# Feed-forward weights from one list in order of use, token sums in the second product, tables one step per block

## The chip, the cores and the metric

The kernel runs on one core of a Trainium2 chip. The metric is the device time of one execution in microseconds (us). A core has a matrix engine (PE, with its weight loads PEld), a vector engine (DVE), a scalar engine (ACT), a general engine (POOL) and an engine that here only issues transfers (SP); each takes its instructions strictly in order, and they meet at semaphores.

## What is computed

Two hybrid layers (a gated delta rule beside sliding-window attention, then a feed-forward part), followed by a state-space block; 512 tokens, width 1024, all in fp32. The change touches the feed-forward part and the tables of the state-space block. Of the reference this is what matters:

```python
D_MODEL, SEQ, DEPTH, D_FF = 1024, 512, 2, 4 * 1024

def hybrid_layer(x, ...):
    ...
    x = x + rmsnorm(mix, post_mix_g)
    h2 = rmsnorm(x, pre_mlp_g)
    ff = jnp.square(jax.nn.relu(h2 @ w_ff1)) @ w_ff2
    return x + rmsnorm(ff, post_mlp_g)
```

The state-space block later needs tables of powers of a complex number per state (exponentials, sines, rotations) that depend on its parameters alone. They can be made at any time before, and the kernel makes half of them beside each layer's feed-forward part.

## The kernel before

**Precision.** Each fp32 operand is split into a high and a low part (`wh`/`wl` for weights, `xsh`/`xsl` for the normed input, `hh`/`hl` for the hidden layer), and a product is three matrix multiplications, high by high, low by high and high by low (`mm3`, L78). For a weight tile of 512 KB that is one transfer from DRAM into `raw` or `raws`, one cast on ACT (L191 or L252) and one subtraction on DVE (L192 or L253). `wh` and `wl` are rings of three, `raw` and `raws` of two each. Kept weights are called `kw`.

**Stages of a feed-forward part.** The 4096 hidden columns come in four blocks of eight columns of 128 (`gidx`); for each block the first product makes the hidden columns, and the second product adds their share to `acc`. In layer 0 the part runs from about 618 to 1000 us of the trace, in layer 1 from about 1612 to 1995.

- Block 0 begins while the residual of the part before still runs: its first six columns (`NFF`) are made in two token halves (`dense_half`, 24 multiplications of 256 columns each), all six for the first half of the tokens, then all six for the second. The second halves need the normed input `xsh`/`xsl` of the second token half, which comes from the residual: load `xo` (SP), `rt` (DVE, POOL), write `xd_mid` (SP), `xsh` (ACT), `xsl` (DVE). Columns 6 and 7 are made as a fast pair.
- A fast pair (`fast_pair`) makes two columns with seven half products in place of eight. It needs sums of weights, formed in `load_pair` on POOL (L257 to L261), each then cast (L252) and subtracted (L253), and sums of tokens `ta`, `tb` (`token_sums`), formed once per layer beside the six second halves. Its results are added up on DVE (`y`, L280).
- Blocks 1 to 3 make their eight columns in four fast pairs each. Blocks 0 to 2 then run the second product over all 512 tokens (`dense2` for two columns, `dense` for six), block 3 in token halves with the residual that follows; its first five weight columns are kept for the second half.

**Tables.** `ssm_tables` is a generator of 38 steps, advanced twice per pair and once per column of a second product. Its prologue loads `row`, `dt` (two transfers of 2 KB in 4-byte pieces), `lbr`, `lbi`; then come an exponential of `dt` on ACT (L1047, with a load of the activation table before it), small DVE steps, seven steps on POOL (six operations of 128x128 each, L1000 to L1005), transposes, loads of `crow` with transposes on PE (L81), and eight steps on DVE (L1000 to L1005).

**What sets the order.** A scheduler takes the instructions in the order in which the program issues them and the buffers' state, and writes one list per engine. All transfers go through SP's queue, on eight semaphores in turn, so a transfer also waits for the one eight places ahead of it.

Of the kernel before, what the change touches and what calls it, by code (L numbers as in the profile page):

```python
# [19 lines left out]
P = 128  # L20
SEQ = 512
# [5 lines left out]
SKIP, KEPT, LATE, FREE, HPOOL = 2, 5, (5, 6, 7, 0, 1, 2, 3, 4), (3, 0, 0, 0), (((0, 0), (1, 0), (2, 0), (3, 0)), ())  # L27
# [27 lines left out]
def body(  # L55
# [118 lines left out]

    def load_w(src, kn=KD, n=P, pool_h=False, keep=None):
        turn[0] += 1
        if turn[0] % 3 == 2 and turn[1] is not None and turn[0] > turn[2]:
            raw = turn[1].tile([P, kn, n], F32, tag="rawx", name="rawx", bufs=1)
        else:
            raw = raw_tile() if kn == KD and n == P else wp.tile([P, kn, n], F32, tag="raw", name="raw", bufs=2)  # L180
# [30 lines left out]
    def dense2(ws, xs):  # L211
        ps = [ps_mm() for _ in ws]
        kn = len(xs)
        order = (*range(kn - 2), kn - 1, kn - 2)
        for ks in (order[:-2], order[-2:]):
            for p, (h, lo) in zip(ps, ws):
                for k in ks:
                    mm3(p, h[:, k, :], lo[:, k, :], *xs[k], k == order[0], k == order[-1])
        return ps
# [18 lines left out]
    def load_pair(src, c, pool):  # L238


        r0, r1 = raw_tile(), raw_tile()
        for j, r in enumerate((r0, r1)):
            DMA.dma_start(out=r, in_=src[:, (c + j) * P:(c + j + 1) * P].rearrange("(k p) n -> p k n", p=P))
        a1, a2 = slice(0, 4), slice(4, 8)
        s1 = pool.tile([P, 4, P], F32, tag="s1", name="s1", bufs=1)

        def parts(raw):
            if raw is s1:
                h, lo = [pool.tile([P, 4, P], F32R, tag=nm, name=nm, bufs=1) for nm in ("sh", "sl")]
            else:  # L250
                h, lo = [wp.tile([P, KD, P], F32R, tag=nm, name=nm, bufs=3) for nm in ("wh", "wl")]
            S.copy(out=h, in_=raw)  # L252
            V.tensor_tensor(out=lo, in0=raw, in1=f32(h), op=ALU.subtract)  # L253
            return h, lo

        d = parts(r0)
        G.tensor_tensor(out=s1, in0=r1[:, a1], in1=r1[:, a2], op=ALU.add)  # L257
        G.tensor_tensor(out=r1[:, a1], in0=r0[:, a1], in1=r1[:, a1], op=ALU.subtract)
        x = parts(r1)
        G.tensor_tensor(out=r0[:, a1], in0=s1, in1=r0[:, a1], op=ALU.subtract)  # L260
        G.tensor_tensor(out=r0[:, a2], in0=r0[:, a2], in1=r0[:, a1], op=ALU.subtract)  # L261
        return d, x, parts(r0), parts(s1)

# [1443 lines left out]
```

## Time and profile before

| | |
|---|---|
| median of 3 runs | 2347.36 us (2345.46 to 2352.49) |
| the profiled execution | 2347.78 us |
| its span | 2346.1 us |
| PE busy | 2241.6 us (96%) |
| DVE, ACT, POOL busy | 1517.7, 955.5, 629.1 us |
| mean granted clock of PE | 0.983 |

The profiled execution is 0.4 us above the median, and 1.7 us of it lie outside the span. A busy PE is not PE at full rate: where the clock is 0.50 a multiplication takes twice as long, and the engine still counts as busy.

### The profile page before, as it was taken

The numbers are of one execution on the slowest core, as the hardware profiler recorded it, in microseconds if no ns is written. First come the engines' busy times: TensorE is split into PE (matmuls) and PEld (weight loads), VectorE is DVE, ScalarE is ACT, GpSimd is POOL, SyncE is SP. The second block draws the span as 40 slices with busy tenths as digits, with TensorE's granted clock in tenths as the row PEclk, the third lists the DMA queues.
The fourth block names the chain that finished last, engine by engine and source line by source line (L and its number), as shares of the span: only waits on it lengthen the run. The fifth ranks groups of instructions, "written<-read, shape, count | busy, mean of one in ns | idle before, by whom it ended". The sixth has DMA issues, their size and how long they took to land. (4 is left out here: it accounts for less than half of the span.)

```text
span 2346.1 us, 37815 instructions
## 1 busy us (share of the span) xinstructions
PE 2241.6 (96%) x14532; PEld 1953.5 (83%) x14532; DVE 1517.7 (65%) x2976; ACT 955.5 (41%) x1734; POOL 629.1 (27%) x683
## 2 busy tenths in 40 slices
PE   8999999999989999999999999999899999899998
PEld 7877888888978888988778888789788899877788
DVE  5579793446677685665797934467776866544645
ACT  4454333233543353444543333335433434424333
POOL 1644320200417123246443202004271232200001
PEclk9999999999989999999999999999999999999999
DMA  6232424665442433342223345654434324554344
GB/s 178 57 78 83 96 81 128 178 205 168 140 111 84 119 109 94 107 138 59 73 83 93 94 127 181 201 158 140 111 92 120 112 73 140 175 162 121 100 135 144
DMA packets 466432, 284.34 MB, mean 121 GB/s; under 512 B 48502, under 2 KB 440012, under 8 KB 465740
## 3 DMA queue, kind: packets, MB, share of 16 engines
q1 hardware_dynamic: 464848, 281.74, 41.4%
q8 instruction: 114, 1.87, 0.3%
q14 instruction: 66, 0.54, 0.1%
q10 hardware_dynamic: 1404, 0.19, 0.1%
HBM read 235.76 MB, written 46.11 MB: 120 GB/s over the span
## 5 line engine op out<-in xcount | busy, mean ns | idle before, releaser
L78 PE MATMUL psm<-xsh,wh 128*128 128x512 f32 (+1 forms) x1104 | 431.9, 392 | 1.4 <-ACT xsh L307 1.0
L78 PE MATMUL psm<-xsl,wh 128*128 128x512 f32 (+1 forms) x1104 | 418.7, 379 | 4.3 <-DVE xsl L310 3.9
L78 PE MATMUL psm<-xsh,wl 128*128 128x512 f32 (+1 forms) x1104 | 419.0, 380 | 0.0
L192 DVE TENSOR_TENSOR wl<-raw,wh 128x1024 fp32r<-128x1024 f32 (+2 forms) x207 | 252.9, 1222 | 110.3 <-ACT wh L191 81.8
L191 ACT CAST wh<-raw 128x1024 fp32r<-128x1024 f32 (+2 forms) x154 | 152.9, 993 | 316.8 <-PE psm L78 254.9
L78 PEld LDWEIGHTS psm<-xsh,wh 128*128 128x128 f32 x1104 | 210.3, 191 | 44.5 <-issue 7.6
L78 PEld LDWEIGHTS psm<-xsl,wh 128*128 128x128 f32 x1104 | 210.9, 191 | 40.3 <-DVE xsl L310 4.6
L78 PEld LDWEIGHTS psm<-xsh,wl 128*128 128x128 f32 x1104 | 210.1, 190 | 40.0 <-issue 0.3
L341 POOL TENSOR_TENSOR sa<-sa,sq 128x256 f32<-128x256 f32 x54 | 51.8, 960 | 659.4 <-ACT sq L336 375.0
L78 PE MATMUL psm<-hh,wh 128*128 128x512 f32 (+1 forms) x480 | 177.6, 374 | 0.0
L78 PE MATMUL psm<-hl,wh 128*128 128x512 f32 (+1 forms) x480 | 176.6, 369 | 0.0
L78 PE MATMUL psm<-hh,wl 128*128 128x512 f32 (+1 forms) x480 | 175.6, 369 | 0.0
L78 PE MATMUL psa<-tb,wh 128*128 128x256 f32 x416 | 82.2, 295 | 25.0 <-ACT wh L252 20.7
L78 PEld LDWEIGHTS psm<-hh,wh 128*128 128x128 f32 x480 | 90.3, 189 | 15.7 <-ACT wh L191 0.8
L78 PEld LDWEIGHTS psm<-hh,wl 128*128 128x128 f32 x480 | 90.5, 188 | 15.2
L78 PEld LDWEIGHTS psm<-hl,wh 128*128 128x128 f32 x480 | 90.5, 189 | 14.9 <-issue 0.8
L189 POOL TENSOR_SCALAR wh<-raw 128x1024 fp32r<-128x1024 f32 (+1 forms) x53 | 61.5, 1162 | 151.7 <-PE psm L78 120.1
L78 PEld LDWEIGHTS psa<-tb,wh 128*128 128x128 f32 x416 | 68.0, 201 | 26.9 <-ACT wh L252 21.5
L78 PE MATMUL psa<-xsh,wh 128*128 128x256 f32 x312 | 89.1, 286 | 0.0
L78 PE MATMUL psa<-xsl,wh 128*128 128x256 f32 x312 | 88.9, 285 | 0.0
L78 PE MATMUL psa<-xsh,wl 128*128 128x256 f32 x312 | 88.9, 285 | 0.0
L78 PE MATMUL psm<-ah,wh 128*128 128x512 f32 x256 | 80.8, 396 | 5.7 <-ACT ah L307 5.2
(672 smaller groups left out, 5726.0 us busy)
## 6 DMA issues: line engine op xcount, KB each, us to landing
raw<-in_w_in_dram SPq DMA_DIRECT2D x130, 512.0 KB, 3.9
raw<-in_w_ff_dram SPq DMA_DIRECT2D x75, 512.0 KB, 4.3
raws<-in_w_ff_dram SPq DMA_DIRECT2D x49, 512.0 KB, 4.0
gate<-dg SPq DMA_DIRECT2D x48, 256.0 KB, 3.8
rawx<-in_w_in_dram SPq DMA_DIRECT2D x14, 512.0 KB, 4.1
raw<-in_w_up_sw_dram SPq DMA_DIRECT2D x12, 512.0 KB, 5.1
raw<-in_w_up_dn_dram SPq DMA_DIRECT2D x11, 512.0 KB, 6.6
raw<-in_w_o_dram SPq DMA_DIRECT2D x10, 512.0 KB, 5.2
```

Source lines behind the costliest of these rows:

```text
L78: return s.issue(nc.tensor.matmul(*a, **k))
L189: G.tensor_scalar(out=h, in0=raw, scalar1=1.0, scalar2=0.0, op0=ALU.mult, op1=ALU.add)
L191: S.copy(out=h, in_=raw)
L192: V.tensor_tensor(out=lo, in0=raw, in1=f32(h), op=ALU.subtract)
L341: (G if s.n in POOL_ACC else V).tensor_tensor(out=s.acc, in0=s.acc, in1=sq, op=ALU.add)
```

## The change

- A class `Weights` holds one list of the feed-forward weights in order of use. It starts the preparation of the next weight (transfer, sums, cast, subtraction) in the program as soon as a place in its ring is released, after the last product that reads it (`free`), where before `load_w` and `load_pair` stood directly before the use. With the list, transfers run up to one item ahead.
- Columns 6 and 7 of block 0 are plain products over all 512 tokens (48 multiplications of 512 columns) and no longer a fast pair (84 of 256 columns).
- The token sums are issued in the second product of block 0, one step per column; their pool is opened after the six columns are done.
- The tables advance once per pair or column, after it, and no longer twice per pair; `crow` is loaded some steps earlier, in two buffers.
- In block 3 the first three columns' weights come from the list; two columns are kept in place of five, so columns 0, 1 and 2 are loaded and split a second time in the second token half, at its end.

```diff
-SKIP, KEPT, LATE, FREE, HPOOL = 2, 5, (5, 6, 7, 0, 1, 2, 3, 4), (3, 0, 0, 0), (((0, 0), (1, 0), (2, 0), (3, 0)), ())
+SKIP, KEPT, LATE, FREE, HPOOL = 2, 5, (5, 6, 7, 3, 4, 0, 1, 2), (3, 0, 0, 0), (((0, 0), (1, 0), (2, 0), (3, 0)), ())
...
+    class Weights:
+        def __init__(s, items):
+            s.items, s.fetched, s.got = list(items), [], []
+            s.steps = [(i, p) for i, (src, pair) in enumerate(s.items) for p in ("dxes" if pair else "w")]
+            s.room = {"ring": 0, "s": 1}
...
+        def fetch(s, upto):
+            while len(s.fetched) <= min(upto, len(s.items) - 1):
+                src, pair = s.items[len(s.fetched)]
+                raw = []
+                for j in range(1 + pair):
+                    raw.append(raw_tile())
+                    DMA.dma_start(out=raw[j], in_=src[:, j * P:(j + 1) * P].rearrange("(k p) n -> p k n", p=P))
+                s.fetched.append(raw)
...
+        def free(s, what):
+            s.room[what] += 1
+            while s.steps and s.room["s" if s.steps[0][1] == "s" else "ring"]:
+                i, p = s.steps.pop(0)
+                s.room["s" if p == "s" else "ring"] -= 1
+                s.fetch(i)
+                s.got.append(s.part(p, s.fetched[i]))
+                if spare[0] is not None and p in "ws":
+                    s.fetch(i + 1)
...
+        def part(s, p, raw):
...
+            elif p == "x":
+                G.tensor_tensor(out=s.s1, in0=raw[1][:, a1], in1=raw[1][:, a2], op=ALU.add)
+                G.tensor_tensor(out=raw[1][:, a1], in0=raw[0][:, a1], in1=raw[1][:, a1], op=ALU.subtract)
+            elif p == "e":
+                G.tensor_tensor(out=raw[0][:, a1], in0=s.s1, in1=raw[0][:, a1], op=ALU.subtract)
+                G.tensor_tensor(out=raw[0][:, a2], in0=raw[0][:, a2], in1=raw[0][:, a1], op=ALU.subtract)
...
+            S.copy(out=h, in_=t)
+            V.tensor_tensor(out=lo, in0=t, in1=f32(h), op=ALU.subtract)
+            return h, lo
...
-        tR = sp.tile([P, NG, 32], F32, tag="crow", name="tR")
+        tR = sp.tile([P, NG, 32], F32, tag="crow", name="tR", bufs=2)
...
+            items = [up(n) for n in range(NFF, KD)]
+            for g in range(4):
+                if g:
+                    items += [up(g * KD + n, 2) for n in range(0, KD, 2)]
+                items += [down(g, n) for n in range(KD if g < 3 else 3)]
+            w = Weights(items)
...
-                            ts = next(sums, None) or ts
+                        if i and n < 3:
+                            w.free("ring")
...
-                    ys = fast_pair(load_pair(w_ff1[l], gidx * KD + len(hid), spare[0]), mid.xs, ts)
-                    for _ in range(2):
-                        next(tables, None)
...
+                    if gidx:
+                        ys = fast_pair(w, mid.xs, ts)
...
+                    else:
+                        ps = dense(w.take(), mid.xs)
+                        w.free("ring")
+                        hid.append(hidden())
+                        relu2(ps, *hid[-1])
+                    next(tables, None)
...
                         if gidx == 0:
                             V.tensor_copy(out=acc[n], in_=ps)
+                            next(sums, None)
...
-                return kp.tile([P, kn, n], F32R, tag="kw", name="kw", bufs=10)
+                return kp.tile([P, kn, n], F32R, tag="kw", name="kw", bufs=4)
...
+                    if i == 0 and n < 3:
+                        wn = w.take()
+                    elif i and j > 4:
+                        wn = load_w(down(3, n)[0])
```

How the order on the engines moves at three places of layer 0 (layer 1 has the same at its place):

On SP, before, the prologue of the tables (`row`, `dt`, `lbr`, `lbi`) stands behind the last loads of the token sums (`tsa`, `tsb`), after the whole residual:

```order
L290 DMA tsa_6712<-xd_mid0_5569 128x512
L290 DMA tsb_6713<-xd_mid0_5569 128x512
L243 DMA raws_6812<-in_w_ff1_dram 128x8x128
L1030 DMA row_6934<-in_ssm_lam_re_2_dram 8x128
L1038 DMA dt_6946<-in_ssm_log_dt_2_dram 64x8x1 x2
L1043 DMA lbr_6949<-in_ssm_b_re_2_dram 64x8x16 x2
L1043 DMA lbi_6950<-in_ssm_b_im_2_dram 64x8x16 x2
L181 DMA raws_6993<-in_w_ff2_dram 128x8x128
```

On SP, after, the same transfers stand within the residual of the second token half, between its fourth load (`xo_6344`) and its first write (`xd_mid0<-rt_6314`), with weight loads between them:

```order
L430 DMA xo_6344<-xd_in_96 128x256
L1059 DMA row_6798<-in_ssm_lam_re_2_dram 8x128
L1067 DMA dt_6810<-in_ssm_log_dt_2_dram 64x8x1 x2
L1072 DMA lbr_6813<-in_ssm_b_re_2_dram 64x8x16
L231 DMA raw_6230<-in_w_ff1_dram 128x8x128
L1072 DMA lbr_6813<-in_ssm_b_re_2_dram 64x8x16
L1072 DMA lbi_6814<-in_ssm_b_im_2_dram 64x8x16
L189 DMA raw_6562<-in_w_ff1_dram 128x8x128
L1072 DMA lbi_6814<-in_ssm_b_im_2_dram 64x8x16
L401 DMA xd_mid0_5569<-rt_6314 128x256
L430 DMA xo_6355<-xd_in_96 128x256
L189 DMA raw_6599<-in_w_ff1_dram 128x8x128
```

So the last four `xo` loads of the residual, and the load `raw_6599` of column 7's weight, now stand behind the prologue.

On ACT, before, the exponential of `dt` stands behind the last eviction of the six columns and ahead of the casts for the fast pair:

```order
L307 CAST hh_6501<-fq_6788 128x256
L277 COPY y0_6924<-psa_6836 128x256
L1047 ACT_TABLE_LOAD
L1047 ACTIVATE dt_6946<-dt_6946 128x8
L252 CAST sh_6832<-s1_6815 128x512
L252 CAST wh_6822<-raws_6812 128x1024
L252 CAST wh_6828<-raw_6811 128x1024
L191 CAST wh_6995<-raws_6993 128x1024
```

On ACT, after, it stands ahead of the first eviction of the six columns (`ft_6263` from `psm_6238`), and so ahead of every `xsh` of the second token half:

```order
L365 ACTIVATE sq_6190<-mo_5568 128x256
L241 CAST kw_6226<-raw_6224 128x1024
L1076 ACT_TABLE_LOAD
L1076 ACTIVATE dt_6810<-dt_6810 128x8
L1380 ACTIVATE ft_6263<-psm_6238 128x256
L1382 ACTIVATE fq_6265<-ft_6263 128x256
L336 CAST hh_6236<-fq_6265 128x256
L241 CAST kw_6232<-raw_6230 128x1024
L1380 ACTIVATE ft_6303<-psm_6278 128x256
L1382 ACTIVATE fq_6305<-ft_6303 128x256
L336 CAST hh_6276<-fq_6305 128x256
L341 ACTIVATE xsh_5922<-rt_6314,prm_91 128x256
```

The exponential has moved over some 45 instructions of ACT, from behind the second halves to ahead of the first.

Further down on ACT, after, the casts of the weights of columns 6 and 7 (`wh_6564`, `wh_6601`) stand among the evictions of the second halves:

```order
L336 CAST hh_6465<-fq_6494 128x256
L1380 ACTIVATE ft_6525<-psm_6500 128x256
L320 ACTIVATE tsa_6983<-tsa_6983,prm_91 128x512
L320 ACTIVATE tsb_6984<-tsb_6984,prm_91 128x512
L1382 ACTIVATE fq_6527<-ft_6525 128x256
L221 CAST wh_6564<-raw_6562 128x1024
L1380 ACTIVATE ft_6556<-psm_6531 128x256
L336 CAST hh_6498<-fq_6527 128x256
L1382 ACTIVATE fq_6558<-ft_6556 128x256
L336 CAST hh_6236<-fq_6558 128x256
L221 CAST wh_6601<-raw_6599 128x1024
```

There, `psm_6531` is the first of the six second halves, so both casts come some five columns ahead of the products that read them.

## Rows read from the trace of the kernel before

**Rows 1.** PE's waits, layer 0, 640 to 1040 us: total us, times, longest.

```profile
PE psa L78 <- ACT wh L252: 11.8, 2, 9.7
...
PE psa L81 <- DMA crow<-in_ssm_c_im_dram: 2.8, 1, 2.8
...
PE psm L78 <- DVE kw L192: 2.4, 1, 2.4
...
PE psa L78 <- DVE y L280: 1.9, 2, 1.5
```

**Rows 2.** PE's waits, layer 1, 1640 to 2060 us.

```profile
PE psa L78 <- ACT wh L252: 8.9, 2, 6.7
...
PE psa L81 <- DMA crow<-in_ssm_c_im_dram: 2.6, 1, 2.6
PE psm L78 <- DVE kw L192: 2.3, 1, 2.3
```

**Rows 3.** Timeline of PE: start, us, instruction, idle before and its releaser.

```profile
668.62 0.79 PE L78 MATMUL psa<-tb,wh 128*128 128x256 f32 x2 [9.66 <-ACT wh L252]
...
1661.58 0.80 PE L78 MATMUL psa<-tb,wh 128*128 128x256 f32 x2 [6.68 <-ACT wh L252]
```

**Rows 4.** Stretches: us, busy time per engine, PEclk, DMA share, GB/s.

```profile
662.00:664.00 2.00, 0.00 (x0) 0.00 (x0) 1.99 (x3) 0.38 (x1) 1.32 (x1) 0.50 0.14 9
...
674.00:676.00 2.00, 2.00 (x16) 2.00 (x16) 0.16 (x1) 1.05 (x1) 0.00 (x0) 0.78 1.05 309
...
820.00:830.00 10.00, 9.50 (x67) 9.53 (x68) 9.34 (x31) 2.37 (x3) 2.22 (x2) 0.83 0.19 54
...
1950.00:1960.00 10.00, 9.82 (x69) 9.82 (x70) 6.36 (x8) 6.43 (x10) 0.00 (x0) 0.83 0.63 185
```

**Rows 5.** Timeline of ACT at the first stall of layer 0.

```profile
663.62 1.28 ACT L1047 ACT_TABLE_LOAD   x1 [4.08 <-DMA dt<-in_ssm_log_dt_dram]
666.90 0.21 ACT L1047 ACTIVATE dt<-dt 128x8 f32<-128x8 f32 x1 [2.00 <-DMA dt<-in_ssm_log_dt_dram]
```

**Rows 6.** Timeline of SP: the last xo loads, then the tables' prologue.

```profile
632.77 0.94 SPq L401 DMA_DIRECT2D xo<-xd_in  x2
...
654.52 1.37 SPq L1038 DMA_DIRECT2D dt<-in_ssm_log_dt_dram  x2
...
657.29 7.80 SPq L1043 DMA_DIRECT2D lbi<-in_ssm_b_im_dram  x2
```

**Rows 7.** Timeline of ACT and of PE where the residual meets the first halves.

```profile
622.01 0.38 ACT L1347 ACTIVATE ft<-psm 128x256 f32<-128x256 f32 x1
...
640.51 0.49 ACT L312 ACTIVATE xsh<-rt,prm 128x256 fp32r<-128x256 f32 x1
...
618.93 0.28 PE L78 MATMUL psm<-xsh,wh 128*128 128x256 f32 x1
...
629.34 0.28 PE L78 MATMUL psm<-xsh,kw 128*128 128x256 f32 x1
629.46 0.28 PE L78 MATMUL psm<-xsl,kw 128*128 128x256 f32 x1
```

**Rows 8.** Timeline of PE in a second product: neighbouring multiplications of 512 columns.

```profile
690.76 0.39 PE L78 MATMUL psm<-hh,wh 128*128 128x512 f32 x1
690.99 0.39 PE L78 MATMUL psm<-hl,wh 128*128 128x512 f32 x1
```

**Rows 9.** Block 1 of layer 0: a stretch, and DVE groups of 725 to 766.

```profile
730.00:740.00 10.00, 10.00 (x86) 10.00 (x85) 3.46 (x8) 2.41 (x3) 9.61 (x19) 1.00 0.34 98
...
L253 DVE TENSOR_TENSOR wl<-raw,wh 128x1024 fp32r<-128x1024 f32 x6 | 9.4, 1560 | 10.1 <-ACT wh L252 10.1
```

**Rows 10.** The page's fifth part: DVE's subtractions and ACT's casts, whole span.

```profile
L192 DVE TENSOR_TENSOR wl<-raw,wh 128x1024 fp32r<-128x1024 f32 (+2 forms) x207 | 252.9, 1222 | 110.3 <-ACT wh L191 81.8
L191 ACT CAST wh<-raw 128x1024 fp32r<-128x1024 f32 (+2 forms) x154 | 152.9, 993 | 316.8 <-PE psm L78 254.9
```

More of the change, by code (lines that the diff above doesn't have):

```diff
@@ L209, in dense, with dense2 @@
         return ps
-    def dense2(ws, xs):
-        ps = [ps_mm() for _ in ws]
+    def dense2(w, xs):
+        ps, ws = [ps_mm() for _ in range(2)], [w.take() for _ in range(2)]
         kn = len(xs)
@@ L236, in dense_half @@
         return ps
[L238 to L262, printed above, removed]
     def fast_pair(w, xs, ts):
-        (d, x, y, z), p1, p2 = w, slice(0, HS), slice(HS, SEQ)
+        p1, p2 = slice(0, HS), slice(HS, SEQ)
         ps = [ps_ax((P, SEQ)) for _ in range(4)]
@@ L1095, in ssm_tables @@
         yield
+        crows = []
+        for src in (ssm_c_re_2, ssm_c_im_2):
+            crow = sp.tile([P, 2, 2, 64], F32, tag="crow", name="crow", bufs=2)
+            for dup in range(2):
+                DMA.dma_start(out=crow[:, :, dup, :], in_=src[0, grs].rearrange("(q g) c p -> (g c) q p", q=2))
+            crows.append(crow)
         s16 = (P, NG, 16)
@@ L1124, in ssm_tables @@
         for dst, src in ((wre, ssm_c_re_2), (wni, ssm_c_im_2)):
-            crow = tl("crow", (P, 2, 2, 64))
-            for dup in range(2):
-                DMA.dma_start(out=crow[:, :, dup, :], in_=src[0, grs].rearrange("(q g) c p -> (g c) q p", q=2))
+            crow = crows.pop(0)
             for q in range(2):
@@ L1358, in layer @@
                 tick = ticks(pending, AT_FF)
-                wk = [load_w(w_ff1[l][:, n * P:(n + 1) * P], keep=keep if n >= 3 else None) for n in range(NFF)]
+                wk = [load_w(up(n)[0], keep=keep if n >= 3 else None) for n in range(NFF)]
                 for i in range(2):
@@ L1388, in layer @@
                 while len(hid) < KD:
[L1389 to L1402 removed]
+                    if gidx:
+                        ys = fast_pair(w, mid.xs, ts)
+                        new = [hidden(), hidden()]
+                        for y, hl in zip(ys[::-1], new[::-1]):
+                            relu2(y, *hl)
+                        hid += new
+                    else:
+                        ps = dense(w.take(), mid.xs)
+                        w.free("ring")
+                        hid.append(hidden())
+                        relu2(ps, *hid[-1])
+                    next(tables, None)
                 if gidx < 3:
[L1405 removed]
+                    first = dense2(w, hid)
                     for n in range(KD):
[L1407 to L1408 removed]
+                        ps = first[n] if n < 2 else dense(w.take(), hid)
+                        if n >= 2:
+                            w.free("ring")
                         if gidx == 0:
                             V.tensor_copy(out=acc[n], in_=ps)
+                            next(sums, None)
                         else:
                             V.tensor_tensor(out=acc[n], in0=ps, in1=acc[n], op=ALU.add)
+                        next(tables, None)
+            finish(tables)
+            spare[0] = None
+            es2.close()
+            tr = tail.enter_context(sbuf(f"tr{l}", "right"))
             xst = Stream(nxt[0], nxt[1], f"xd_out{l}", tr, True)
```

71 lines of the change are left out of this document (37 added, 34 removed).

## The prediction

> **What bounds the kernel now.** PE is busy 96% of the span, so a change can gain only what PE idles, and what it loses at the lower clock. I read first PE's list of waits over the feed-forward part of each layer [rows 1, 2]: the reader is to see that one entry, a wait for ACT's casts `wh` of a fast pair, holds half of the sum, and in each layer nearly all of it is one wait. The timeline gives its places [rows 3]: 9.66 us at 668.62, 6.68 us at 1661.58, both where the six columns of block 0 are done and the first fast pair begins. Next I read the granted clock there [rows 4]: it is 0.50 while PE idles, and 0.78 in the stretch from 674 to 676, where it returns. That is 1.2 GHz in place of 2.4 while PE is already working. At 0.78, 0.9 of these 2 us were still slow, so PE worked at half rate from 668.6 to 674.9 and lost half of it, 3.1 us.
>
> Then the cause. ACT stands still 4.08 us and 2.00 us for `dt` [rows 5] and only then casts what PE waits for. The `dt` pair is issued from 654.52 [rows 6] and the second has landed at 666.90: 12.4 us for 4 KB. In the same time SP needs 7.80 us to issue the two `lbi` [rows 6], and the DMA engines' mean share is 0.14 [rows 4]. So it is not bandwidth; it is the small pieces of these transfers, in ACT's and SP's in-order queues ahead of the weights.
>
> **The change part by part.** All against the profiled execution, 2347.8 us, which is 0.4 above the median.
>
> 1. *The first stall goes.* In the changed order the casts of columns 6 and 7 stand among the evictions of the second halves, about five half columns ahead of their use, and the products are of another form, so nothing of the fast pair is waited for. I count 9.7 + 3.1 = 12.8 us in layer 0 and 6.7 + 3.1 = 9.8 in layer 1, taking layer 0's clock loss for both. What is late next is the weights of the second product; its casts follow on the same list, with six half columns (24 multiplications each, 0.12 apart [rows 7], 2.9 us each) to cover them.
>
> 2. *`crow` is loaded earlier*, ahead of the POOL steps, while its transposes stay in place: 2.8 and 2.6 us [rows 1, 2] go. In layer 0 the clock is 0.83 over the following 10 us [rows 4]: 3.4 us at half rate, 1.7 lost. Layer 1 gets no clock term. 4.5 + 2.6.
>
> 3. *The first weights of block 3's second product come from the list.* The wait for `kw` goes, 2.4 and 2.3 us, with a clock loss of 1.7 each, by the stretch from 1950 to 1960 at 0.83 [rows 4]: 4.1 + 4.0.
>
> 4. *The eight DVE steps of the tables* (numbers 27 to 34 of 38) move from the pairs of block 2 into its second product, where DVE adds once per column and no longer per half product. The wait for `y`, 1.9 us in layer 0 [rows 1] and counted alike for layer 1, goes: 1.9 + 1.9.
>
> Sum of the gains: 12.8 + 4.5 + 4.1 + 1.9 = 23.3 in layer 0, 9.8 + 2.6 + 4.0 + 1.9 = 18.3 in layer 1; 41.6.
>
> 5. *Block 0 without its fast pair:* 48 multiplications of 512 columns at 0.23 apart [rows 8] are 11.0 us, 84 of 256 at 0.12 [rows 7] are 10.1. Cost 0.9 per layer, all on PE. The pair's POOL sums, casts and subtractions fall away beside it.
>
> 6. *The new wait.* The prologue of the tables now stands in the residual of the second token half: on SP ahead of its last four `xo`, on ACT ahead of the first eviction of the six columns. Its first transfer waits for the end of the output projection, which is when the first half column starts, 618.9 [rows 7]. With 0.8 us for `row` and 12.4 from the first `dt` issue to the second landing, ACT could load its table at 631.8; with 9.1 (the first `dt`, 654.52 to 663.62 [rows 5, 6]), at 628.5. Then 1.28 + 0.21 [rows 5] and the eviction's 0.38 [rows 7], which before ran at 622.01. Matrix results of the halves have three buffers, so the fourth half column, which began at 629.34 [rows 7], needs that eviction: it begins at 630.4 to 633.7, 1.0 to 4.3 us late. I take 3.5, nearer the longer end, since both `dt` are needed; not the end itself, since before a weight of 512 KB was issued directly ahead of `dt`, and now nothing large is. Behind it on ACT stand three evictions and the cast of `kw_6232`; behind its subtraction on DVE (the weight buffer's release) waits `raw_6599` on SP, and behind that the last three `xo`. The eviction ends at 632.9, then two ACT steps of its size, a cast of 1.0 and a subtraction of 1.2 [rows 10]: 635.9. Six issues of 0.47 [rows 6] bring the last `xo` to 638.7. From the last `xo` issue to the end of the last `xsh` it was 633.7 to 641.0 [rows 6, 7], 7.3 us: 646.0. PE, 3.5 late, is at the last piece of its first second half at 644.1. So 1.9 more, 5.4 in all, and half of the 1.7 that a stall of 2.8 us cost in clock: 6.3 per layer. Bounds 1 (the short landing, later parts covered) and 12 (the `lbi` landing holds the last `xo` as well).
>
> A rule of the Trainium skill bears on this: the page "DMA: Bandwidth & Descriptors", section "Queues, rings and completion order", says that a DMA engine consumes the descriptors of a queue in ring order. The trace agrees in so far as SP's issue of `lbi` stood 7.80 us while few engines moved anything [rows 4, 6]. By that rule `raw_6230`, now between the two `lbr`, lands behind the small pieces; the cast that it feeds stands behind the table load anyway, so the sum would come out about 2 us per layer higher, near 2331, and without it stays.
>
> 7. *Block 1.* The seven POOL steps of the tables (42 operations) still stand among the sums of its first pairs in the changed order. POOL is 9.61 of 10 busy there [rows 9] and PE waits 11.8 - 9.7 = 2.1 us for casts [rows 1]. DVE's subtractions of 1024 columns take 1.56 us there [rows 9] against 1.22 over the span [rows 10]. Bounds: -5 (these waits and their clock go) to +6 (the second pair's last sum stands behind some 21 table operations). I take +1.5 per layer, as the pairs start earlier against the same POOL work.
>
> 8. *Block 0's second product and block 3's last half.* The token sums come on top of the table steps on DVE and ACT in the one; three more loads, casts and subtractions [rows 10] per layer in the other, beside the residual. Each is 0 to 2 us; PE has eight columns of 24 x 0.23 = 5.5 us for cover in the one and five half columns in the other. Together +1.5 per layer.
>
> Costs: 2 x (0.9 + 6.3 + 1.5 + 1.5) = 20.4. Net 41.6 - 20.4 = 21.2: 2347.8 - 21.2 = 2326.6, and on the median's scale 2326.
>
> **The rivals.**
>
> *A, the new wait eats the gain.* The `dt` landing and the issue of `lbi` act one after the other on the residual: SP's list has `lbr`, `lbi`, and after them `xo` loads that wait for the landing of each on its semaphore. If the last `xo` goes out 12.4 + 7.8 us after 619.7, with lbi's own landing of some 9 us behind, it is at 649, the last `xsh` at 656, against 641 for PE: 15 us, and with the clock's 3.1 some 18 per layer in place of 6.3, and block 1 at its upper bound, +6. Then 2326.6 + 23.4 + 9 = 2359. The point from which it is slower: the new wait at 6.3 + 21.2/2 = 17 us per layer. For it: the same prologue cost 12.8 us in its old place. Against: at 619 no weight of 512 KB is issued directly ahead of it, and the first halves run on for some 20 us from there.
>
> *B, the prologue is hidden.* `dt` lands in 9 us or less, the later parts fit, block 1's waits shrink: cost per layer 0.9 + 1 + 0.5, block 1 at -4. 2347.8 - 41.6 + 4.8 - 8 = 2303.
>
> *C, block 1 gives it back.* The weights of the pairs are requested at release, but POOL still has the tables first: +6 and a clock of 3.1 in block 1 of each layer, and the new wait at 8: 2326.6 + 2 x (7.6 + 1.7) = 2345, no change. The Trainium skill speaks for it: "GPSIMD Engine Reference", section "1. Specifications", has POOL's SBUF interfaces shared with DVE's instructions that have two SBUF inputs; the 1.56 against 1.22 agrees.
>
> *D, the list doesn't do what it says.* Preparation is issued at release, but the engines' lists put it late again, behind token sums that wait for `xd_mid`; half of the first stall stays: 2326.6 + 11 = 2338. The order speaks against it.
>
> **How the numbers follow.** Forecast 0.52, A 0.10, B 0.15, C 0.13, D 0.10. The range leaves out most of A and half of B: 2306 to 2346. What a measurement can tell from no change here is about 0.3%, 7 us, so "same" is 2340 to 2354. Faster: the forecast, B, D and a little of C, 0.77. Same: most of C and the mild end of A, 0.15. Slower: 0.08.
>
> **What would show it.** In the changed profile: no long wait for `wh` near the start of block 0's second product; ACT idle for `dt` near 622 to 632 and PE waiting for evictions or `xsh` between 629 and 647; no wait for `crow`; none for `kw` near 957; block 1's waits for `wh` and `wl` within 2 us of before. I am wrong if the residual's new wait is over 12 us per layer, if block 1's POOL stretch grows, or if ACT waits for `dt` cost PE nothing.

## The result

| | median | ratio to the kernel before (95% interval) |
|---|---|---|
| the kernel before | 2346.41 us, 4 runs (2344.59 to 2352.49) | |
| the changed kernel | 2323.51 us, 4 runs (2320.57 to 2324.69) | 0.9896 (0.9876 to 0.9917) |

The change gains 1.0%, 23 us (19 to 29 by the interval); the forecast was 2326. The profiled execution has a span of 2321.4 us, 24.7 less than before.

PE is busy 2238.8 us after and 2241.6 before, so most of what was gained is idle time. First PE's waits after, in layer 0 from the start of the feed-forward part to the first norm sum of the residual behind it (618 to 966 us), against [rows 1]. Columns: total us, times, longest.

```profile
PE psm L78 <- ACT ft L1380: 3.4, 1, 3.4
PE psa L78 <- DVE wl L222: 2.6, 3, 1.0
PE psa L78 <- ACT wh L221: 1.3, 2, 1.0
PE psm L78 <- DVE xsl L342: 1.1, 2, 0.9
...
```

The same list of layer 1 (1601 to 1952 us), against [rows 2].

```profile
PE psm L78 <- ACT ft L1380: 3.3, 1, 3.3
PE psm L78 <- ACT hh L336: 2.9, 1, 2.9
PE psa L78 <- DVE wl L222: 2.7, 3, 1.1
PE psm L78 <- DVE xsl L342: 2.6, 3, 1.4
PE psa L78 <- ACT wh L221: 1.3, 2, 1.0
...
```

The waits of 9.7 and 6.7 us for `wh`, those for `crow`, `kw` and `y` are gone. In their place stand a wait for an eviction (`ft`) and for `xsl`, in both layers, and in layer 1 one for `hh`. By parts of the program, each from one norm sum to another (`ones,sa` on PE), the time went here:

| us | before | after | difference | forecast |
|---|---|---|---|---|
| layer 0, feed-forward part to the end of its residual | 411.7 | 392.9 | -18.8 | -13.1 |
| layer 1, the same | 410.2 | 403.1 | -7.1 | -8.1 |
| the rest | 1524.2 | 1525.4 | +1.2 | 0 |

Within a layer, each product from its first multiplication to that of the next product, in us. Layer 0 before and after, and layer 0 of the experiments below (there "dt row" is the first, "pair" the one with the fast pair back, "cut" the one without POOL's steps, "DVE" the last):

| product | before | after | dt row | pair | cut | DVE |
|---|---|---|---|---|---|---|
| block 0 first | 60.4 | 55.4 | 48.3 | 55.7 | 49.6 | 49.2 |
| block 0 second | 45.0 | 44.5 | 44.5 | 45.0 | 44.5 | 44.5 |
| block 1 first | 47.6 | 47.0 | 47.0 | 46.9 | 40.3 | 44.5 |
| block 1 second | 48.8 | 44.4 | 44.5 | 44.0 | 44.5 | 44.5 |
| block 2 first | 44.3 | 41.4 | 41.3 | 41.6 | 41.3 | 41.3 |
| block 2 second | 49.1 | 43.9 | 43.9 | 44.0 | 43.9 | 43.9 |
| block 3 first | 40.4 | 44.7 | 44.9 | 44.5 | 44.9 | 44.9 |

Block 2's second product lost 5.2 us and block 3's first gained 4.3: work of the tables on PE moved from the one to the other.

The new wait, in the timelines after. On SP, the transfers of the tables' prologue and the residual's loads, against [rows 6]:

```profile
618.41 1.37 SPq L1067 DMA_DIRECT2D dt<-in_ssm_log_dt_dram  x2
...
622.40 5.85 SPq L1072 DMA_DIRECT2D lbr<-in_ssm_b_re_dram  x1
628.30 2.30 SPq L1072 DMA_DIRECT2D lbi<-in_ssm_b_im_dram  x1
...
631.31 2.92 SPq L1072 DMA_DIRECT2D lbi<-in_ssm_b_im_dram  x1
...
635.83 0.43 SPq L430 DMA_DIRECT2D xo<-xd_in  x1
...
639.91 0.98 SPq L430 DMA_DIRECT2D xo<-xd_in  x2
```

The 4-byte pieces of `dt` hold the transfers behind them, too. The weight `raw` was issued at 621.95, but the DMA engines moved next to nothing until 628 (last numbers: their share, GB/s):

```profile
626.00:628.00 2.00, 2.00 (x20) 2.00 (x19) 0.00 (x0) 0.00 (x0) 0.00 (x0) 1.00 0.04 0
628.00:630.00 2.00, 1.47 (x13) 1.26 (x11) 0.00 (x0) 0.00 (x0) 0.00 (x0) 1.00 0.37 67
```

On ACT, against [rows 5], and the first eviction and last `xsh` against [rows 7]:

```profile
631.02 1.28 ACT L1076 ACT_TABLE_LOAD   x1 [8.97 <-DMA dt<-in_ssm_log_dt_dram]
632.32 0.21 ACT L1076 ACTIVATE dt<-dt 128x8 f32<-128x8 f32 x1
632.43 0.37 ACT L1380 ACTIVATE ft<-psm 128x256 f32<-128x256 f32 x1
...
646.80 0.49 ACT L341 ACTIVATE xsh<-rt,prm 128x256 fp32r<-128x256 f32 x1
```

And on PE, with the clock behind it in the stretches of 2 us (the columns of [rows 4]):

```profile
632.85 0.39 PE L78 MATMUL psm<-xsh,kw 128*128 128x256 f32 x1 [3.39 <-ACT ft L1380]
...
647.61 0.38 PE L78 MATMUL psm<-xsl,wh 128*128 128x256 f32 x1 [0.89 <-DVE xsl L342]
...
634.00:636.00 2.00, 2.00 (x12) 2.00 (x11) 1.69 (x3) 1.94 (x5) 0.73 (x1) 0.50 0.55 118
636.00:638.00 2.00, 2.00 (x14) 2.00 (x14) 2.00 (x6) 1.19 (x4) 0.99 (x2) 0.72 0.53 153
```

ACT stands for 8.97 us, every other instruction behind it; the fourth half column is 3.39 us late, and the clock falls to half for some 3 us, which costs 1.6. In layer 1 the same wait, 3.3 us, ended at 1611.5 and the clock stayed at 1.00; there it fell only at about 1627, behind the waits for `xsl`:

```profile
1612.00:1614.00 2.00, 2.00 (x19) 2.00 (x19) 1.32 (x3) 1.88 (x4) 0.70 (x1) 1.00 0.97 176
...
1628.00:1630.00 2.00, 2.00 (x11) 2.00 (x11) 1.09 (x3) 0.46 (x1) 0.39 (x1) 0.50 0.74 192
```

### The profile page after: what moved, and what is told of

Read it like the earlier page. It is cut to its first block, busy times and chain, and to the rows that moved or that the text cites. A ratio compares the mean times of both kernels' runs of the same rounds, so it can differ in the third digit from the quotient of the medians.

```text
span 2321.4 us, 37699 instructions
## 1 busy us (share of the span) xinstructions
PE 2238.8 (96%) x14460; PEld 1951.9 (84%) x14460; DVE 1502.6 (65%) x2964; ACT 957.4 (41%) x1734; POOL 616.0 (27%) x675
## 5 line engine op out<-in xcount | busy, mean ns | idle before, releaser
L242 DVE TENSOR_TENSOR wl<-raw,wh 128x1024 fp32r<-128x1024 f32 (+3 forms) x187 | 226.3, 1212 | 101.3 <-ACT wh L241 74.0
L78 PEld LDWEIGHTS psm<-xsh,wl 128*128 128x128 f32 x1136 | 217.6, 192 | 41.4 <-issue 0.3
L241 ACT CAST wh<-raw 128x1024 fp32r<-128x1024 f32 (+3 forms) x134 | 131.8, 984 | 259.5 <-PE psm L78 222.9
L78 PE MATMUL psm<-hh,wh 128*128 128x512 f32 (+1 forms) x576 | 204.5, 359 | 2.9 <-ACT hh L336 2.9
L78 PE MATMUL psm<-hl,wh 128*128 128x512 f32 (+1 forms) x576 | 205.1, 357 | 0.1
L78 PE MATMUL psm<-hh,wl 128*128 128x512 f32 (+1 forms) x576 | 204.3, 357 | 0.0
L221 ACT CAST wh<-raw 128x1024 fp32r<-128x1024 f32 x67 | 70.2, 1050 | 131.0 <-PE psm L78 78.1
L221 ACT CAST wh<-raws 128x1024 fp32r<-128x1024 f32 x63 | 65.9, 1046 | 133.4 <-PE psm L78 76.8
L222 DVE TENSOR_TENSOR wl<-raw,wh 128x1024 fp32r<-128x1024 f32 x67 | 98.1, 1465 | 24.4 <-ACT wh L221 24.3
L222 DVE TENSOR_TENSOR wl<-raws,wh 128x1024 fp32r<-128x1024 f32 x63 | 90.1, 1431 | 23.1 <-ACT wh L221 23.0
L339 DVE TENSOR_TENSOR hl<-fq,hh 128x512 fp32r<-128x512 f32 (+1 forms) x76 | 57.5, 759 | 41.5 <-ACT hh L336 41.4
```

What stands on the lines that cost most here:

```text
L78: return s.issue(nc.tensor.matmul(*a, **k))
L221: S.copy(out=h, in_=t)
L222: V.tensor_tensor(out=lo, in0=t, in1=f32(h), op=ALU.subtract)
L339: V.tensor_tensor(out=lo, in0=src, in1=f32(hi), op=ALU.subtract)
```

## The experiments

The kernel before took 2338 to 2343 us on the chips of these runs, so ratios to it are compared, and otherwise stretches of the feed-forward parts. Where nothing was edited, the products of blocks 1 to 3 agree between runs within 0.1 us in most cases and about 1 at worst; block 0's first product differs by up to 1.4 us, and what follows block 3's first product by up to 3.

### The step sizes as one row

```diff
-        for half in range(2):
-            DMA.dma_start(out=dt[64 * half:64 * half + 64, :],
-                          in_=ssm_log_dt_2[0, grs].rearrange("(i two) -> two i", two=2)[half].partition_broadcast(64))
+        drow = sp.tile([1, 2 * NG], F32, tag="drow", name="drow")
+        DMA.dma_start(out=drow, in_=ssm_log_dt_2[0:1, grs])
+        psd = ps_ax((P, 2 * NG))
+        T.matmul(psd, lhsT=ones[0:1, :], rhs=drow, start=True, stop=True)
...
-        S.activation(out=dt, in_=dt, func=AF.Exp)
+        for half in range(2):
+            hs = slice(64 * half, 64 * half + 64)
+            S.activation(out=dt[hs], in_=psd[hs, half::2], func=AF.Exp)
```

> The changed kernel, with the step sizes dt loaded as one row of 64 bytes and spread over the partitions by one small product with ones, in place of two transfers of 512 pieces of 4 bytes; nothing else. Theory (the small pieces of dt are what holds ACT in the residual, 8.97 us, and so PE, 3.4 us for the eviction and 1.3 for xsl): the wait for the eviction goes in both layers, and with it most of the clock loss, about 5 us per layer: 2313. Rival one (the two lbi transfers, which stay in SP's queue, delay the xo loads just as much): the eviction's wait goes, the wait for xsl grows to 3 or more, 2 to 3 us per layer: 2318. Rival two (PE had slack, the wait comes back at the end of the residual): 2323.

Measured: 2304.33 us, 0.9845 (0.983 to 0.986), against 0.9896 for the change. The feed-forward parts are 8.4 and 9.2 us shorter than after the change, 7.1 and 7.6 of it in block 0's first product; the rest lies behind block 3's first product, where nothing was edited. PE's waits in layer 0, 618 to 960 us:

```profile
PE psa L78 <- ACT wh L221: 1.9, 1, 1.9
PE psa L78 <- DVE wl L222: 1.9, 2, 1.1
```

Neither an eviction nor `xsl` is waited for. SP, with the `lbi` transfers still there:

```profile
623.01 1.29 SPq L1073 DMA_DIRECT2D lbi<-in_ssm_b_im_dram  x2
...
633.08 0.97 SPq L430 DMA_DIRECT2D xo<-xd_in  x2
```

The two `lbi` are now issued in 1.29 us, and the last `xo` goes out 7 us earlier. So the theory holds in kind, with more gained than its 5 us per layer, and more is shown than expected: SP's long issues are not `lbi`'s own cost but the queue behind `dt`'s 1024 pieces. Rival one falls. The edit also lets the scheduler place the exponential later, in block 0's second product, so it isn't only the shorter landing that is tried here; the next run shows that moving the whole prologue removes the residual's wait as well.

### The pools in the other order

```diff
-            sums = token_sums(mid, es2.enter_context(sbuf(f"ts{l}")), ts)
             tables = ssm_tables(es2.enter_context(sbuf(f"st{l}")), l)
+            sums = token_sums(mid, es2.enter_context(sbuf(f"ts{l}")), ts)
```

> The changed kernel, with the pools of the tables and of the token sums opened in the other order, so that the tables' prologue waits for the memory of the kept weights and stands behind the six columns again, as before the change. Theory (the first stall went because the fast pair of block 0 went; dt in front of ACT's work costs the two plain columns little, since PE has 11 us of products without ACT): the new wait of the residual goes (6 us per layer), 1 to 3 us come back near the end of columns 6 and 7: 2314 to 2318. Rival (the first stall went because dt was moved out of its place): 8 to 10 us come back per layer: 2328 to 2335.

Measured: 2317.95 us, 0.9907 (0.9889 to 0.9925), no different from the change. The prologue stands behind the six columns again, so which of the two pools is opened first decided where it stands; that it is the memory each then gets is the reading of it. Block 0's first product took 48.8 us in layer 0 (55.4 after the change) and 48.7 in layer 1 (56.8): the residual's wait is gone and the first stall did not come back. The rival falls. But of the theory's 1 to 3 us that were to come back, 8.0 and 7.5 came: block 0's second product is 2.9 and 3.8 us longer, block 1's first 5.1 and 3.7. PE's longest waits of 665 to 766 us in layer 0, all in block 1, show it (a wait of 1.6 us for the second `row` stands in block 0's second product):

```profile
PE psa L78 <- DVE wl L222: 4.5, 4, 1.5
PE psa L78 <- ACT wh L221: 3.1, 2, 2.4
...
```

That the later prologue pushes the tables' steps into block 1 is read from the order.

### The kernel before with the one row

The same diff on the kernel before.

> The kernel before, with dt loaded as one row as in the run on the changed kernel; nothing else. Theory (of the first stall of 9.66 us in layer 0, dt in ACT's queue is the last part; POOL's sums for the pair end near 663.4, and the casts would follow): PE goes on at about 664.5 in place of 668.6, with less time at the low clock: 5 to 6 us less in layer 0 and 2 to 5 in layer 1: 2337 to 2340. Rival one (dt is all of it): 12 and 9 us less, 2326. Rival two (the pair's weights are all of it, dt only overlaps): within 2 us, 2345.

Measured: 2337.56 us, 0.9983 (0.9974 to 0.9993), 4 us less. The feed-forward parts are 4.4 and 1.0 us shorter. The first stall in layer 0 and layer 1:

```profile
659.99 0.80 PE L78 MATMUL psa<-tb,wh 128*128 128x256 f32 x2 [3.00 <-ACT wh L252]
...
663.41 0.58 PE L78 MATMUL psa<-tb,wl 128*128 128x256 f32 x1 [2.62 <-DVE wl L253]
...
1652.03 0.80 PE L78 MATMUL psa<-tb,wh 128*128 128x256 f32 x2 [5.14 <-ACT wh L252]
```

5.6 us in place of 10.1 in layer 0 (9.66 and 0.47 for the first `wl`), and in layer 1 5.9 in place of 7.1. So `dt` was about half of the stall in layer 0 and little of it in layer 1. The rest is not the same in the two layers. In layer 0 of this run ACT waits for the pair's sums of weights on POOL, 1.76 us before the second cast. In layer 1 ACT of the kernel before, which the prediction had not looked at, never waited for `dt`; it waited for a step of the token sums (`tsb`), ahead of the pair's second cast on its list:

```profile
1656.19 0.62 ACT L307 CAST tb<-tsb 128x512 fp32r<-128x512 f32 x1 [3.24 <-DVE tsb L295]
...
1658.82 1.28 ACT L1047 ACT_TABLE_LOAD   x1
```

With the one row this wait stays, 3.15 us.

### Late loads of `crow`, the tables at the old pace, and both

The loads of `crow` directly ahead of their transposes, in one buffer, with the rest of the change:

```diff
-            crow = crows.pop(0)
+            crow = tl("crow", (P, 2, 2, 64))
+            for dup in range(2):
+                DMA.dma_start(out=crow[:, :, dup, :], in_=src[0, grs].rearrange("(q g) c p -> (g c) q p", q=2))
```

> The changed kernel, with the two loads of crow put back directly ahead of their transposes, in one buffer; nothing else. Theory (the early load is what removed PE's wait for crow): a wait for crow of 2.5 to 3 us comes back in each layer, with 1.7 of clock in one of them: 2323.5 + 7 = 2330. Rival (the transposes themselves moved, and the load has cover anyway): 2324.

Measured: 2320.79 us, 0.9918 (0.9899 to 0.9937). No wait for `crow` in either layer; the feed-forward parts are 1.4 and 0.1 us longer, the 1.4 in block 0's first product. The theory falls, the rival holds. Then the pace:

```diff
-                    next(tables, None)
+                    for _ in range(2):
+                        next(tables, None)
```

> The changed kernel, with the tables advanced twice per pair or column of a first product, as before the change, and once per column of a second product; nothing else. Theory (one step per pair took the eight DVE steps out of block 2's pairs, and with them the wait for y and, since the early load of crow alone did not matter, the wait for crow): a wait for y near 1.9 us and one for crow of about 2.7 come back in each layer, block 1 as it is: 2323.5 + 8 to 10 = 2332. Rival (y and crow were late because of the pairs' own weights, which now come from the list): within 2 us of 2323.5.

Measured: 2330.78 us, 0.9957 (0.994 to 0.9974); the feed-forward parts are 6.4 and 6.9 us longer. Block 1's second product grew by 1.5, block 2's first by 5.0, its second by 2.2 us, and block 3's first shrank by 4.5. PE's waits from 760 to 970 us:

```profile
PE psa L78 <- DVE wl L222: 2.5, 2, 1.8
PE psm L78 <- ACT hh L336: 1.7, 1, 1.7
PE psa L78 <- DVE y L310: 0.5, 1, 0.5
```

In each layer 4.2 us of it lie in these four products and 2.1 and 1.5 at the start of block 3's second product, with the wait for `hh`. So the pace is worth some 6 us per layer. It is DVE in block 2's pairs, as forecast, though more of it shows as a wait for `wl` than for `y`. No wait for `crow` here either. Both edits together:

> The changed kernel, with the tables advanced twice per pair and the loads of crow directly ahead of their transposes, as before the change in both; each edit alone brought no wait for crow. Theory (either part alone covers the second load of crow: the early load, or the slower pace that puts the transposes into a product of 512 columns): PE waits 2.5 to 2.8 us for crow in each layer in block 1's second product, beside what the pace alone cost. Rival (the list's transfers changed the queue, and crow is covered anyway): no such wait.

Measured: 2325.21 us, 0.9931 (0.9911 to 0.995). Still no wait for `crow`. The theory falls. `crow`'s transposes and its second load in layer 0:

```profile
796.05 0.38 PE L81 MATMUL psa<-ident,crow 128*128 128x128 f32 x2
802.67 0.38 PE L81 MATMUL psa<-ident,crow 128*128 128x128 f32 x2
...
L1156 SPq DMA_DIRECT2D crow<-in_ssm_c_im_dram x2: 368/416/463, 796.5 to 796.9; - x2
```

Before, the second pair of transposes stood directly behind the first on PE and waited 2.8 us for a load issued between them [rows 1]. Here the load is as late, but the pair comes 6.6 us after the first, behind products. So the distance on PE covers the load. Neither of these two runs has quite the pace of before, though: block 0's two columns advance the tables four times here, where one pair did it twice, so the step of `crow`, number 26, falls on the sixth column of block 1's second product, and before on the eighth, its last, with no product of the block behind it. After the change it falls on the last pair of block 2. That the place at the product's end made the wait is read from these counts and was not run.

### Block 3's second product as before

```diff
-                items += [down(g, n) for n in range(KD if g < 3 else 3)]
+                items += [down(g, n) for n in range(KD if g < 3 else 0)]
...
-                    if i == 0 and n < 3:
-                        wn = w.take()
-                    elif i and j > 4:
-                        wn = load_w(down(3, n)[0])
-                    elif i:
+                    if i:
                         wn = wk[n]
```

> The changed kernel, with block 3's second product as before the change: all its weights by load_w directly ahead of their use, five kept columns in place of two, no second load of columns 0, 1 and 2. Theory (the list removed the wait for kw, 2.4 us and 1.7 of clock per layer; the second loads cost the tail of layer 0 a part of the 0.9 us and layer 1 of the 2.0 us that the tails grew): the wait for kw comes back in each layer and in layer 1 the 2.87 us for hh goes, while the tails shrink by 1 to 2 us each: within 4 us of the changed kernel, 2323 to 2327 where the changed kernel is 2323.5. Rival (the tails pay for the list): 2318.

Measured: 2322.11 us, 0.9925 (0.9898 to 0.9952). The wait for `kw` came back in both layers, longer than before:

```profile
940.62 0.58 PE L78 MATMUL psm<-hh,kw 128*128 128x256 f32 x1 [3.52 <-ACT kw L241]
...
1921.76 0.38 PE L78 MATMUL psm<-hh,kw 128*128 128x256 f32 x1 [3.52 <-ACT kw L241]
```

The theory holds for each wait. Up to the residual layer 0 is 6.7 us longer and layer 1 unchanged, where the wait for `hh` went in exchange; the residuals behind are 1.1 and 2.9 us shorter. So the list is worth its second loads in layer 0 and costs 3 us in layer 1.

With the one row as well:

> The changed kernel with dt as one row of 64 bytes, as in the run that gave 2304 on a chip where the kernel before took 2343, and block 3's second product as before the change. Theory (the two edits touch stages that are 300 us apart and add up): the difference to the run with dt as one row is that of the run with block 3 as before to the changed kernel, within 2 us. Rival (with more room in the tables' stage the last block's order shifts too): more than 4 us apart.

Measured: 2309.24 us, 0.9865 (0.9842 to 0.9888). Against the one row alone, layer 0 is 8.3 us longer and layer 1 0.6 shorter; against the change, the edit alone gave 5.6 longer and 2.9 shorter. Over both layers that is 7.7 against 2.7 us, 5 apart, the rival's side; by the ratios it is 4.7 against 6.8, with intervals too wide to decide. That the two edits add up is not shown.

### The fast pair back in block 0

```diff
-            items = [up(n) for n in range(NFF, KD)]
+            items = [up(NFF, 2)]
...
+            for _ in range(3):
+                w.free("ring")
             for gidx in range(4):
```

The token sums, which a pair needs, stand beside the second halves again, and the list starts only when the pool of the raw tiles is open.

> The changed kernel, with block 0's columns 6 and 7 as a fast pair again, whose weights come from the list as soon as the pool of the raw tiles is open (after the six columns), and with the token sums back beside the second halves; nothing else. With it the exponential of dt falls back behind the six columns, after three of the pair's casts. Theory (the pair's chain of transfer, sums on POOL and casts is what the first stall was made of, and the plain columns removed it): a wait for wh at the first pair of 3 to 6 us comes back in each layer, and the new wait of the residual goes (6 us): 2320 to 2328. Rival one (the list alone suffices): no such wait, 2311. Rival two (all of the old stall comes back): 2330 to 2335.

Measured: 2320.31 us, 0.9914 (0.9892 to 0.9935). The first pair's waits in layers 0 and 1:

```profile
662.32 0.58 PE L78 MATMUL psa<-xsh,wh 128*128 128x256 f32 x1 [5.73 <-ACT wh L221]
...
1642.99 0.80 PE L78 MATMUL psa<-tb,wh 128*128 128x256 f32 x2 [6.81 <-ACT wh L221]
```

The stall comes back in the theory's size, but not for its reason. ACT's casts for the pair stand behind the token sums and the last evictions, and in layer 1 ACT waits there for `tsb`, as in the kernel before; POOL had ended the sum that the second cast (1641.90) needs at 1637.1:

```profile
1639.11 0.62 ACT L336 CAST tb<-tsb 128x512 fp32r<-128x512 f32 x1 [3.11 <-DVE tsb L324]
```

So the list, as early as it can start here, does not remove the stall; columns that need no token sums do. Block 0's first product takes 55.7 us with the pair and 55.4 with the plain columns in layer 0, 58.2 and 56.8 in layer 1: most of what they saved was given to the new wait in the residual.

### The tables advanced at another pace

Twice per column of block 0's second product, and not in the pairs of blocks 2 and 3, with the one row (the first place is the loop of the first products, the second that of the second products):

```diff
-                    next(tables, None)
+                    if gidx < 2:
+                        next(tables, None)
...
                         if gidx == 0:
                             V.tensor_copy(out=acc[n], in_=ps)
                             next(sums, None)
+                            next(tables, None)
```

> The changed kernel with dt as one row, and the tables advanced twice per column of block 0's second product and not at all in the pairs of blocks 2 and 3, so that the seven POOL steps may start earlier. Theory (POOL's table steps in front of the pairs' sums are what is left of block 1's waits, and POOL is free in block 0's second product): block 1's first product goes from 47.0 to 44 or 45 us in each layer, 4 to 6 us in all, against 2304 on the chip where the kernel before took 2343. Rival (DVE's small steps, which come ahead of the POOL steps, take block 0's second product anyway): within 2 us.

Measured: 2310.84 us, 0.987 (0.9855 to 0.9885), slower than the one row alone (the feed-forward parts are 5.8 and 5.5 us longer). Block 1's first product grew to 50.3 us, with a wait of 2.5 us for `y`, and block 2's second to 48.9, while block 3's first shrank to 40.3. Neither theory nor rival: POOL's seven steps began at 700.42, 11.1 us ahead of block 1, as they do with the one row alone (701.25, block 1 at 712.30), so what the theory wanted to move stayed and is not tried. What came earlier are the tables' transposes on PE, into block 1's first product, and the eight DVE steps, into its second.

### POOL's table steps cut, then moved to DVE

With the one row:

```diff
-            cmul(ebr[:, :, j, :], ebi[:, :, j, :], bc(are, s16), bc(aim, s16), ebr[:, :, j + 1, :], ebi[:, :, j + 1, :], tD, eng=G)
+            G.memset(ebr[:, :, j, :], 0.0)
+            G.memset(ebi[:, :, j, :], 0.0)
```

> The changed kernel with dt as one row, and the seven POOL steps of the tables replaced by two fills with zero each (the tables are left out for seven of eight powers; the state-space block then computes with zeros). Theory (POOL's 42 operations in front of the pairs' sums hold block 1): block 1's waits for wh and wl, 3.8 us, and their clock go: its first product takes 41.5 to 43 us in place of 47.0, 8 to 11 us in both layers. Rival (the pairs' own chain of transfer, sums, cast and subtraction is longer than PE's time for a pair at the start of a block): the first product stays above 45.

Measured: 2293.75 us, 0.9786 (0.9766 to 0.9807). Block 1's first product takes 40.3 us in both layers, 6.7 less than with the one row, and PE waits for nothing in it. The theory holds. The feed-forward parts as a whole are 4.8 us shorter each; block 0's first product in layer 0 and the stretch behind block 3's first product took some of it back. One stretch of block 1 after the change, one with the steps cut (POOL is the fifth number), and DVE's subtractions there, after and cut:

```profile
720.00:730.00 10.00, 10.00 (x86) 10.00 (x85) 6.01 (x10) 2.37 (x3) 9.69 (x17) 1.00 0.19 54
...
L222 DVE TENSOR_TENSOR wl<-raw,wh 128x1024 fp32r<-128x1024 f32 x6 | 9.6, 1597 | 1.0 <-ACT wh L221 1.0
```

```profile
720.00:730.00 10.00, 10.00 (x85) 10.00 (x85) 8.87 (x12) 6.59 (x11) 4.27 (x5) 1.00 0.37 107
...
L222 DVE TENSOR_TENSOR wl<-raw,wh 128x1024 fp32r<-128x1024 f32 x6 | 9.6, 1596 | 3.0 <-ACT wh L221 2.5 <-PE psa L78 0.6
```

POOL falls from 9.69 to 4.27 of 10; the subtractions take 1.60 us on average in both, so it is the place in POOL's queue that cost, not dearer subtractions. So the steps go to DVE, nothing left out:

```diff
-            cmul(ebr[:, :, j, :], ebi[:, :, j, :], bc(are, s16), bc(aim, s16), ebr[:, :, j + 1, :], ebi[:, :, j + 1, :], tD, eng=G)
+            cmul(ebr[:, :, j, :], ebi[:, :, j, :], bc(are, s16), bc(aim, s16), ebr[:, :, j + 1, :], ebi[:, :, j + 1, :], tD)
```

> The changed kernel with dt as one row, and the seven steps of the tables that POOL did (42 operations) on DVE; nothing is left out. In the order they now stand in block 0's second product, ahead of the pairs' subtractions. Theory (POOL's 42 operations in front of the pairs' sums are block 1's waits; without them block 1's first product took 40.3 us in place of 47.0): block 1's first product takes 40 to 42 us, block 0's second product grows by 0 to 3 us, since DVE is 8 to 10 tenths busy there and takes some 20 us more: 8 to 13 us less than with dt as one row alone, a ratio to the kernel before of 0.979 to 0.981. Rival (DVE's subtractions for the second product come late behind the table steps): block 0's second product grows by as much as block 1 gains, ratio 0.984 to 0.986.

Measured: 2296.96 us, 0.9813 (0.9789 to 0.9837); this version beats both kernels; whether it beats the one row alone the intervals just leave open. Block 0's second product stays at 44.5 us, against the rival; block 1's first takes 44.5 in layer 0 and 44.3 in layer 1, not the theory's 40 to 42: 2.5 and 2.8 of the 6.7 us that the cut took off. PE's waits there:

```profile
PE psa L78 <- ACT y L307: 1.7, 2, 0.9
PE psa L78 <- DVE wl L222: 1.3, 1, 1.3
```

The last of the steps run into the first pair on DVE.

## Why the prediction came out

Point by point, by its steps:

1. *The first stall goes:* right; PE waits for nothing from 650 to 690 us. What it said of the cause was read from ACT in layer 0 alone: there `dt` was half of the stall, the pair's sums of weights the rest; in layer 1 ACT did not wait for `dt`, but for the token sums. The stall came back with the fast pair and its token sums although the list started the weights, so it was the form of the columns, and not the list, that removed it.
2. *`crow`:* the wait went (2.78 and 2.61 us), but the reason given, the earlier load, failed: with the load put back the wait stayed away. The premise that the transposes stay in place was wrong: in layer 0 they moved from the end of block 1's second product (817.34 and 820.50) to the start of block 2's second (851.38 and 857.75), where the pairs are 6.4 us apart on PE.
3. *`kw`:* right in layer 0, where the wait for `acc` of 1.1 us went with it. In layer 1 2.87 us for `hh` and 1.7 of clock behind it took its place, which the prediction had not asked for. ACT shows why: a cast of the next weight stands ahead of the last step of the last pair and waits for its transfer.

```profile
1926.08 1.05 ACT L241 CAST kw<-raw 128x1024 fp32r<-128x1024 f32 x1 [2.43 <-DMA raw<-in_w_ff_dram]
1927.03 0.62 ACT L1382 ACTIVATE fq<-ft 128x512 f32<-128x512 f32 x1
```

4. *`y`:* right in kind, as the run at the old pace shows. In size it was low: from block 1's second product to block 3's first the two layers gained 8.2 and 7.9 us, where steps 2 and 4 counted 6.4 and 4.5. In layer 1 1.4 of the difference is a wait for `wl` in block 2 that went too; most of the rest is PE's own time, which no step counted.
5. *Plain columns, 0.9 us of PE:* not measured by itself. With waits and the clock's loss taken off, block 0's first product is 46.1 us before (60.4 less 11.2 and 3.1) and 47.7 with the one row (48.3 less 0.6), 1.6 more.
6. *The new wait, 6.3 per layer:* the mechanism is right in each part, the sizes of the later parts are not. The eviction was forecast for 632.5 and ran at 632.43; PE was 3.4 us late where 3.5 was taken; the last `xsh` ended at 647.3, forecast 646.0, and PE waited 1.3 us there, 0.9 more than before (forecast 1.9); the clock cost 1.6, not 0.85. Together 5.9 in layer 0; in layer 1 3.3, 2.6 and 1.6, 7.1 after the 0.4 of before. That layer 0 comes within 0.4 of the forecast is luck in part, as the clock and `xsh` missed in opposite directions. The rule weighed in this step, that a DMA engine consumes a queue's descriptors in ring order (the Trainium skill's page "DMA: Bandwidth & Descriptors", section "Queues, rings and completion order"), fits: `raw`, issued at 621.95, moved only from 628 on, behind the 4-byte pieces. The 2 us per layer that it would have added did not come, as the cast of that weight (633.77) did not wait for it.
7. *Block 1, +1.5:* it came out at -0.6 and -0.5; the sign was wrong. The pairs did not wait longer behind POOL's steps than before. That POOL's steps are what holds block 1 was right.
8. *Block 0's second product and the tail, +1.5:* the product runs without a wait (44.5 us are 192 multiplications 0.23 apart), and the tails grew by 0.9 and 2.0.

The sum is nearer than its parts. Layer 0 gained 5.7 more than forecast: 2.1 in block 1, 1.8 in steps 2 and 4, 1.3 at the start of block 3's second product (`acc`), 1.1 in step 8, less 0.6 in block 0's first product. Layer 1's sum is right within 1 us only because errors cancel: step 3, with the unforeseen `hh`, fell 4.9 short and block 0's first product 1.6; block 1 gave 2.0 more than forecast and steps 2 and 4 gave 3.4 more.

Of the rivals, none came. A would have needed a last `xo` at 649, and it went out at 640; B needed a new wait of 1 us in place of 5.9 and 7.1, C a block 1 that grows, where it shrank; and D's half of the first stall is not there.

## What to carry to other kernels

A step hoisted by a scheduler because its memory came free brings its slow transfers with it; look at what stands behind it on the in-order engine and at the queue that it shares, not only at its own length. Before moving such a step, shorten it: the row with a small product on PE gave 7 to 8 us in block 0 of each layer, where moving the step gave nothing in the whole. An engine that is far from busy over the span, as POOL here with 27%, can still hold a stage; replacing its work by fills showed what was to be had in block 1 (6.7 us in each layer), and a change of engine brought 2.5 to 2.8 of them without leaving anything out. And look at the same stall in every layer before naming its cause: layer 1's had another one than layer 0's.

## What the runs showed of the hardware

- Two transfers of 2 KB in 4-byte pieces took 12.4 us to land before and 12.6 after (618.41 to 631.02), although after the change no weight was issued directly ahead. SP then needed 2.3 to 5.9 us for one transfer issued behind them (5.85, 2.30 and 2.92 above), and 0.6 for each `lbi` where `dt` came as one row. A weight issued behind them moved nothing for 6 us.
- In layer 0 a wait of 3.4 us was followed by a clock of 0.50 for some 3 us, and so was one of 2.9 us for `hh` in layer 1; a wait of 3.3 us in layer 1 was not, and the clock stayed at 1.00. So the length of one wait did not tell the clock here.
- Of DVE's 130 subtractions of 1024 columns in the list after the change, the 81 that met no instruction of POOL took 1.20 to 1.23 us each; the other 49 took up to 2.3. Two in layer 0, the second beside a sum of weights on POOL from 751.76 to 753.38:

```profile
748.14 1.23 DVE L222 TENSOR_TENSOR wl<-raw,wh 128x1024 fp32r<-128x1024 f32 x1 [0.34 <-ACT wh L221]
...
752.15 2.31 DVE L222 TENSOR_TENSOR wl<-raws,wh 128x1024 fp32r<-128x1024 f32 x1
```
